# A one-column memset on GpSimd between each two additions of exponentials in a forgetting-attention kernel, their order pinned

## The chip, the cores and the metric

The kernel runs on one core of one Trainium2 chip. The metric is the device time of one execution in microseconds (us); a comparison takes the median of several executions. The engines are named as in the profile: PE is TensorE's matmul, PEld its weight load, DVE is VectorE, ACT is ScalarE, POOL is GpSimd, SP is the engine that issues the DMAs.

## The reference, cut to what matters

One decoder layer: forgetting attention with 16 heads of 64 columns, then a gated feed-forward part, then a norm. The change touches the softmax of the attention alone: for each head and each block of queries, `p = softmax(s)` over the keys, and `o = p @ v`.

```python
s = jnp.einsum('bhqd,bhkd->bhqk', q_blk, k).astype(jnp.float32) * (FOX_HEAD_DIM ** -0.5)
s = s + (c_q[..., :, None] - c_k[..., None, :])
s = jnp.where(pos_k[None, :] <= pos_q[:, None], s, -jnp.inf)
p = jax.nn.softmax(s, axis=-1)
return jnp.einsum('bhqk,bhkd->bhqd', p, v.astype(jnp.float32))
```

Each softmax needs the sum of its exponentials over all keys. That sum is what the changed lines form.

## The kernel before

The 1040 positions (1024 and 16 meta tokens) are worked on in three large stages: the attention (to about 700 us), the first feed-forward product (to about 1260 us), and the second with the final norm. Only the attention is touched.

The attention goes by pairs of heads, p = 0 to 7. A pair has two heads e = 0, 1, and the queries are cut into two blocks of 512 columns, c = 0, 1. Keys stand in tiles of 128 partitions, j = 0 to 8; block c = 0 sees 5 of them, block c = 1 all 9, and a tile on the diagonal is narrower than 512 columns (400, 272, 144, 16).

For one head and block the steps are these. `attn_scores` (L342) multiplies keys and queries on PE into PSUM (S, L356 and L357), copies them with a bias on ACT into a tile sb (L363), masks the diagonal part on POOL (the select, L368), and keeps a running maximum rm of the tiles on DVE (L374, L378, L376). `attn_max` (L381) transposes rm on PE (pm, L387), reduces it on DVE (mc, L389) and spreads it again on PE (pb, L392). `attn_exp` (L395) subtracts the maximum on DVE (L398) and takes the exponential on ACT (L399), in place. `attn_out` (L401) multiplies the exponentials by the values on PE (O, L410), and adds the tiles of a head up on POOL:

```python
for i, (j, s, n, sj) in enumerate(tiles[1:]):
    src = total[e] if i else first
    nc.gpsimd.tensor_tensor(total[e][:n, s:], src[:n, s:], sj, ALU.add)
```

These are the additions (L422): 4 of them for each head with c = 0 and 8 with c = 1, so 24 in a pair of heads and 192 in all. Their results, the tiles t (`total`), go to `attn_sum` (L425), which sums them over partitions on PE (Z, L431); `combine_unit` (L465) divides by that sum and multiplies by the gate.

Beside this, PE runs the projections of the next pair (pj, L189 to L195). Their weights come in 512-column pieces (wraw); ACT rounds a piece to its high part wh (L96) and DVE forms the rest, wl = wraw - wh (L98), which PE waits for. In the last pairs the output projection (`oproj`, L477) takes that place: DVE forms the low parts of the weights (wol, L497) and of the attention's output (ob, L490), and PE multiplies them into acca (L504 to L506).

Nothing in the code fixes the order of instructions as a whole: the strings `first`, `steady`, `before` and `final` (L574 to L577) say in which order the steps are recorded, and a scheduler then places every instruction on its engine by its own estimate of when it can start. Each engine works its instructions off in the order so placed. Two means in the code bind the scheduler: `tc.keep_in_program_order` pins an instruction's place relative to others that are pinned, and `tc.issue_after` makes the instructions recorded in its block stand behind a given one on its engine.

Of the kernel before, what the change touches and what calls it, by code (L numbers as in the profile page):

```python
# [8 lines left out]
F32 = mybir.dt.float32  # L9
F32R = mybir.dt.float32r  # L10
AF = mybir.ActivationFunctionType
ALU = mybir.AluOpType
AX = mybir.AxisListType

P = 128
# [20 lines left out]
def fox_block(ctx, tc, hT, hN, wqkvg, w0f, w0g, wo, w1, w2, g_attn, g_ffn, g_fin, g_q, g_k, b_f, out):  # L36
    nc = tc.nc
    PS = bass.MemoryType.PSUM

    cpool = ctx.enter_context(tc.tile_pool(name="cpool", bufs=1))  # L40
# [2 lines left out]
    nc.scalar.preload_act_table_set(ACT_SET)  # L43
    ident = cpool.tile([P, P], F32, tag="ident", name="ident")
    make_identity(nc, ident)
    epsb = cpool.tile([P, 1], F32, tag="epsb", name="epsb")
    nc.gpsimd.memset(epsb, EPS)

# [31 lines left out]
    def bank(tag, name):  # L80
        return ps.tile([P, 512], F32, tag=tag, name=name, bufs=BANKS[tag])
# [29 lines left out]
    def t512(tag, name, dt=F32):  # L111
        return ap_.tile([P, 512], dt, tag=tag, name=name, bufs=BUFS[tag])
# [15 lines left out]
    for k in range(NK):  # L128
# [8 lines left out]
        g = gA[:, k : k + 1]  # L137
# [263 lines left out]
    def attn_out(p, c):  # L401

        st = state[p]
        po = bank("O", f"O{p}_{c}")
        nt = len(st[0, c][0])
        for i in range(nt):
            for e in range(2):
                j, s, n, sj = st[e, c][0][i]
                r = slice(64 * e, 64 * e + 64)
                nc.tensor.matmul(po[r, s:], lhsT=st["V"][:n, j, r], rhs=sj, start=(i == 0), stop=(i == nt - 1))  # L410
        o_t = t512("cmb", f"o{p}_{c}")
        nc.scalar.copy(o_t, po)

        total = st["t", c] = [t512("cmb", f"t{p}_{c}_{e}") for e in range(2)]
        for e in range(2):
            tiles = st[e, c][0]
            first, s1 = tiles[0][3], tiles[1][1]
            if s1 > 0:
                nc.gpsimd.tensor_copy(total[e][:, :s1], first[:, :s1])
            for i, (j, s, n, sj) in enumerate(tiles[1:]):  # L420
                src = total[e] if i else first
                nc.gpsimd.tensor_tensor(total[e][:n, s:], src[:n, s:], sj, ALU.add)  # L422
        st["o", c] = o_t

    def attn_sum(p, c):  # L425
# [153 lines left out]
    for p in range(-1, NK):  # L579
        for op, *a in (first if p < 0 else steady if p + 2 < NK else before if p + 1 < NK else final).split():  # L580
# [6 lines left out]
            elif op == "P":  # L587
                proj_unit(p + 1, *a)
            elif op == "M":
                attn_max(p, *a)  # L590
            elif op == "Z":
                if p >= a[0]:
                    attn_sum(p - a[0], a[1])
            elif op == "N":
                norm_unit(p + 1, *a)
            elif op == "T":
                stack_unit(p + 1, *a)
            elif op == "F":
                forget_unit()
            elif op == "G":  # L600
                gate_unit(p + 1 - int(p + 1 == NK))
            elif op == "W":
                if p + 2 < NK:
                    st_w[p + 2] = stage_w(p + 2)
            elif op == "O":
                attn_out(p, *a)
            elif op == "L":
                combine_load(p, *a)
            elif op == "C":
                if p >= a[0]:  # L610
                    combine_unit(p - a[0], a[1])
            elif op == "A":
                for _ in range(a[1]):
                    next(og[a[0]])
# [487 lines left out]
```

## Time and profile before

| | us |
|---|---|
| runs, lowest / median / highest of 3 | 1440.89 / 1458.1 / 1458.68 |
| the profiled execution | 1449.52 |
| its span, first to last instruction | 1447.9 |
| POOL busy in the span | 448.4 (31%) |
| DVE busy in the span | 1041.0 (72%) |

The profiled execution is one run of its own: 1.6 us of its time lie around the span, and it stands 8.6 us under the median of the three timed runs and 8.6 us over their lowest. The profile tells for each engine when an instruction began and how long it took, and for an idle engine which instruction's end it was waiting for. An instruction that has begun and is held up by something inside the chip shows as a longer duration, not as idle time.

### The profile page before, as it was taken

The numbers are of one execution on the slowest core, as the hardware profiler recorded it, in microseconds if no ns is written. First come the engines' busy times: TensorE is split into PE (matmuls) and PEld (weight loads), VectorE is DVE, ScalarE is ACT, GpSimd is POOL, SyncE is SP. The second block draws the span as 40 slices with busy tenths as digits, with TensorE's granted clock in tenths as the row PEclk, the third lists the DMA queues.
The fourth block names the chain that finished last, engine by engine and source line by source line (L and its number), as shares of the span: only waits on it lengthen the run. The fifth ranks groups of instructions, "written<-read, shape, count | busy, mean of one in ns | idle before, by whom it ended". The sixth has DMA issues, their size and how long they took to land.

```text
span 1447.9 us, 20369 instructions
## 1 busy us (share of the span) xinstructions
PE 1381.0 (95%) x6699; PEld 1115.0 (77%) x6699; DVE 1041.0 (72%) x1819; ACT 679.2 (47%) x1444; POOL 448.4 (31%) x532
## 2 busy tenths in 40 slices
PE   7999999999999999979798999999999999999996
PEld 7887887878787878757576888888888888876874
DVE  7656666777767777677969677666666765798796
ACT  6455555556555565546545233232233323434535
POOL 4021515252432416152404020111111111596182
PEclk9999999999999999999999999999999999999998
DMA  6343425160706142364643232223333228653344
GB/s 200 107 101 92 126 56 154 40 178 19 198 19 176 42 137 74 86 203 143 227 166 124 75 136 88 106 92 109 109 110 109 95 73 301 223 167 100 90 146 146
DMA packets 103196, 178.85 MB, mean 124 GB/s; under 512 B 16553, under 2 KB 25778, under 8 KB 103090
## 3 DMA queue, kind: packets, MB, share of 16 engines
q1 hardware_dynamic: 103090, 177.55, 38.6%
q8 instruction: 53, 0.87, 0.2%
q14 instruction: 53, 0.43, 0.1%
HBM read 109.46 MB, written 38.54 MB: 102 GB/s over the span
## 4 chain that ended last, share of the span: by engine, by line
PE 72%; DVE 13%; DMA 7%; issue 4%; ACT 2%; SPq 1%; POOL 0%; DVEq 0%; ACTq 0%; POOLq 0%
PE f L726 10%; PE f L728 10%; PE f L727 10%; PE pj L193 5%; PE pj L194 5%; PE pj L195 5%; DMA wraw<-wqkvg 5%; PE O L410 3%; PE y L922 2%; PE y L923 2%; PE y L921 2%; PE S L356 2%; PE S L357 2%; PE pg L445 1%; PE pg L446 1%
## 5 line engine op out<-in xcount | busy, mean ns | idle before, releaser
L193 PE MATMUL pj<-wh,xhb 128*128 128x384 f32 (+1 forms) x512 | 176.2, 346 | 7.2 <-ACT xhb L139 5.9
L368 POOL TENSOR_SCALAR_AFFINE_SELECT sb<-sb 128x128 f32<-128x128 f32 (+2 forms) x160 | 58.5, 368 | 390.7 <-ACT sb L363 383.1
L194 PE MATMUL pj<-wl,xhb 128*128 128x384 f32 (+1 forms) x512 | 175.7, 343 | 0.0
L195 PE MATMUL pj<-wh,xlb 128*128 128x384 f32 (+1 forms) x512 | 172.5, 341 | 0.0
L363 ACT ACTIVATE sb<-S,nb 128x512 f32<-128x512 f32 (+4 forms) x224 | 117.0, 538 | 51.9 <-PE S L357 45.9
L422 POOL TENSOR_TENSOR t<-t,sb 128x512 f32<-128x512 f32 (+4 forms) x160 | 136.9, 877 | 0.0
L805 POOL TENSOR_TENSOR gs<-u,u 128x512 f32<-128x512 f32 x11 | 14.1, 1286 | 382.3 <-DVE u L792 382.3
L398 DVE TENSOR_TENSOR sb<-sb,pb 128x512 f32<-128x512 f32 (+4 forms) x224 | 95.7, 497 | 26.6 <-PE pb L392 26.5
L399 ACT ACTIVATE sb<-sb 128x512 f32<-128x512 f32 (+4 forms) x224 | 94.1, 478 | 40.7 <-DVE sb L398 40.6
L193 PEld LDWEIGHTS pj<-wh,xhb 128*128 128x128 f32 x512 | 97.5, 191 | 11.4 <-ACT xhb L139 6.4
L378 DVE TENSOR_TENSOR rm<-rm,sb 128x512 f32<-128x512 f32 (+4 forms) x160 | 87.0, 544 | 20.4 <-ACT sb L363 8.6
L194 PEld LDWEIGHTS pj<-wl,xhb 128*128 128x128 f32 x512 | 97.7, 191 | 4.2 <-issue 2.4
L195 PEld LDWEIGHTS pj<-wh,xlb 128*128 128x128 f32 x512 | 97.1, 190 | 1.5
L410 PE MATMUL O<-sb,V 128*64 128x512 f32 (+4 forms) x448 | 91.9, 463 | 0.0
L356 PE MATMUL S<-Q,K 128*128 128x512 f32 (+4 forms) x224 | 76.2, 344 | 0.7 <-ACT sb L363 0.6
L357 PE MATMUL S<-Q,K 128*128 128x512 f32 (+4 forms) x224 | 71.3, 323 | 0.0
L98 DVE TENSOR_TENSOR wl<-wraw,wh 128x512 fp32r<-128x512 f32 x56 | 48.9, 884 | 30.7 <-ACT wh L96 30.3
L96 ACT CAST wh<-wraw 128x512 fp32r<-128x512 f32 (+1 forms) x64 | 38.5, 607 | 62.7 <-DMA wraw<-wqkvg 32.0
L410 PEld LDWEIGHTS O<-sb,V 128*64 128x64 f32 (+1 forms) x448 | 33.9, 135 | 34.5 <-issue 20.7
L772 DVE TENSOR_TENSOR u<-f,x 128x512 f32<-128x512 f32 x19 | 13.1, 692 | 64.6 <-PE f L728 64.6
L356 PEld LDWEIGHTS S<-Q,K 128*128 128x128 f32 (+1 forms) x224 | 39.5, 176 | 20.7 <-issue 6.5
L374 DVE TENSOR_TENSOR rm<-sb,sb 128x400 f32<-128x400 f32 (+1 forms) x32 | 36.8, 1150 | 24.4 <-ACT sb L363 21.3
(1374 smaller groups left out, 3928.1 us busy)
## 6 DMA issues: line engine op xcount, KB each, us to landing
Q<-tq SPq DMA_DIRECT2D x128, 128.0 KB, 2.3
wraw<-wqkvg SPq DMA_DIRECT2D x56, 256.0 KB, 4.7
av<-w SPq DMA_DIRECT2D x22, 512.0 KB, 3.2
gs<-qs SPq DMA_DIRECT2D x44, 256.0 KB, 2.6
ga<-qa SPq DMA_DIRECT2D x33, 256.0 KB, 3.3
K<-tk SPq DMA_DIRECT2D x64, 128.0 KB, 2.8
wor<-wo SPq DMA_DIRECT2D x32, 256.0 KB, 3.1
a11r<-w SPq DMA_DIRECT2D x22, 256.0 KB, 3.0
```

The lines of the kernel that those rows point to most:

```text
L193: nc.tensor.matmul(o, lhsT=xh[k][:, sl], rhs=wh, start=(k == 0), stop=False)
L194: nc.tensor.matmul(o, lhsT=xh[k][:, sl], rhs=wl, start=False, stop=False)
L195: last_mm[0] = nc.tensor.matmul(o, lhsT=xl[k][:, sl], rhs=wh, start=False, stop=(k == NK - 1))
L356: nc.tensor.matmul(psx[:n, s0:], lhsT=kk[:, j * P : j * P + n], rhs=q[:, 0, s0:], start=True, stop=False)
L357: nc.tensor.matmul(psx[:n, s0:], lhsT=kk[:, j * P : j * P + n], rhs=q[:, 1, s0:], start=False, stop=True)
L363: nc.scalar.activation(sj, psx[:n, s:], AF.Identity, bias=nbias[c][:n, j, head : head + 1], scale=1.0)
L398: nc.vector.tensor_tensor(sj, sj, mx[:n, s:], ALU.subtract)
L410: nc.tensor.matmul(po[r, s:], lhsT=st["V"][:n, j, r], rhs=sj, start=(i == 0), stop=(i == nt - 1))
L422: nc.gpsimd.tensor_tensor(total[e][:n, s:], src[:n, s:], sj, ALU.add)
L726: nc.tensor.matmul(pp, lhsT=s[0][:, ks], rhs=bh, start=(k == 0), stop=False)
L727: nc.tensor.matmul(pp, lhsT=s[0][:, ks], rhs=bl, start=False, stop=False)
L728: nc.tensor.matmul(pp, lhsT=s[1][:, ks], rhs=bh, start=False, stop=(k == 3))
```

## The change

Before each of the 192 additions a memset of one column (128 partitions, one float32 each) is issued on POOL, into a tile `gap` that nothing reads. The memsets are pinned in program order among themselves, and each addition is bound to stand behind its memset.

```diff
+    gap = cpool.tile([P, 1], F32, tag="gap", name="gap")
...
             for i, (j, s, n, sj) in enumerate(tiles[1:]):
                 src = total[e] if i else first
-                nc.gpsimd.tensor_tensor(total[e][:n, s:], src[:n, s:], sj, ALU.add)
+
+                g = tc.keep_in_program_order(nc.gpsimd.memset(gap, 0.0))
+                with tc.issue_after(g.ins):
+                    nc.gpsimd.tensor_tensor(total[e][:n, s:], src[:n, s:], sj, ALU.add)
```

Lines behind the first new one move down by one, lines behind the additions by four: the addition is L426 in the changed kernel, the select L369, wl L98 becomes L99, wol L497 becomes L501, ob L490 becomes L494, rm L374 becomes L375.

The first place is POOL, at the additions of block c = 1 of the first pair of heads. A name t_1_0 is the total of block 1 and head 0, t_1_1 that of head 1; the sb tiles are the exponentials (second input) or, in a select, scores of a later block. In square brackets stand the semaphores that an instruction waits for; Pool_49 is POOL's own. Before:

```order
L422 TENSOR_TENSOR t_1_0_1684<-sb_1_0_1093,sb_1_1_1098 128x512
L422 TENSOR_TENSOR t_1_1_1685<-sb_1_0_1302,sb_1_1_1307 128x512 [waits PE_49]
L422 TENSOR_TENSOR t_1_0_1684<-t_1_0_1684,sb_1_2_1103 128x512 [waits Pool_49]
L368 AFFINE_SELECT sb_0_0_1563<-sb_0_0_1563 128x112 [waits Activation_49]
L422 TENSOR_TENSOR t_1_1_1685<-t_1_1_1685,sb_1_2_1312 128x512 [waits Pool_49]
L368 AFFINE_SELECT sb_0_0_1815<-sb_0_0_1815 128x112 [waits Activation_49]
L422 TENSOR_TENSOR t_1_0_1684<-t_1_0_1684,sb_1_3_1108 128x512 [waits Pool_49]
L422 TENSOR_TENSOR t_1_1_1685<-t_1_1_1685,sb_1_3_1317 128x512 [waits Pool_49]
```

The same place in the changed kernel:

```order
L424 MEMSET gap 128x1
L426 TENSOR_TENSOR t_1_0_1693<-sb_1_0_1094,sb_1_1_1099 128x512
L424 MEMSET gap 128x1 [waits Pool_49]
L426 TENSOR_TENSOR t_1_0_1693<-t_1_0_1693,sb_1_2_1104 128x512 [waits Pool_49]
L424 MEMSET gap 128x1 [waits Pool_49]
L369 AFFINE_SELECT sb_0_0_1572<-sb_0_0_1572 128x112 [waits PE_49,Activation_49]
L426 TENSOR_TENSOR t_1_0_1693<-t_1_0_1693,sb_1_3_1109 128x512 [waits Pool_49]
L424 MEMSET gap 128x1 [waits Pool_49]
L369 AFFINE_SELECT sb_0_0_1840<-sb_0_0_1840 128x112 [waits Activation_49]
L426 TENSOR_TENSOR t_1_0_1693<-t_1_0_1693,sb_1_4_1114 128x512 [waits Pool_49]
```

Before, the two heads' totals alternate, so that an addition waits for the one before the last. Now all eight additions of head 0 come first and then all eight of head 1, and each reads what the addition just in front of it (but for the memset) has written.

The second place is PE, where the sums over partitions of block c = 1 of the second pair of heads stand (Z_1, L431 before and L435 now). Before:

```order
L357 MATMUL S_1_1_2955<-Q_0_1_2702,K_0_2411 128x512
L431 MATMUL Z_1_2853<-t_1_0_2614,one 64x512
L194 MATMUL pj_4_3018<-wl_5_2665,xhb 128x384
L431 MATMUL Z_1_2853<-t_1_1_2615,one 64x512
L356 MATMUL S_1_2_2960<-Q_0_1_2702,K_0_2411 128x512
```

Now, in two pieces with 29 rows between them:

```order
L358 MATMUL S_1_3_3014<-Q_0_1_2751,K_0_2444 128x512
L435 MATMUL Z_1_2902<-t_1_0_2647,one 64x512
L411 MATMUL O_0_3152<-sb_0_0_2526,V_1887 64x512
```

```order
L358 MATMUL S_1_5_3027<-Q_0_1_2751,K_0_2444 128x400
L435 MATMUL Z_1_2902<-t_1_1_2648,one 64x512
L194 MATMUL pj_4_3067<-wh_0_2683,xhb 128x384
```

The sum of head 0 stands 32 rows earlier on PE than before (row 1099 against 1131), that of head 1 four rows earlier (1129 against 1133).

The third place is DVE, near the end of the attention, where the fourth piece of the output projection's weights (wol_0_3) is split. Before:

```order
L490 TENSOR_TENSOR ob_7389<-ogr_3_7559,ob_7389 128x512
L374 TENSOR_TENSOR rm_0_7139<-sb_0_0_7143,sb_0_1_7151 128x400
L378 TENSOR_TENSOR rm_0_7139<-rm_0_7139,sb_0_2_7159 128x272
L497 TENSOR_TENSOR wol_0_3_7566<-wor_0_3_7563,woh_0_3_7565 128x512
L378 TENSOR_TENSOR rm_0_7139<-rm_0_7139,sb_0_3_7167 128x144
```

Now:

```order
L494 TENSOR_TENSOR ob_7558<-ogr_3_7728,ob_7558 128x512
L501 TENSOR_TENSOR wol_0_3_7735<-wor_0_3_7732,woh_0_3_7734 128x512
L375 TENSOR_TENSOR rm_0_7292<-sb_0_0_7296,sb_0_1_7304 128x400
L379 TENSOR_TENSOR rm_0_7292<-rm_0_7292,sb_0_2_7312 128x272
L377 COPY rm_0_7292<-sb_0_0_7296 128x112
```

The split of wol_0_3 stood behind the first two steps of a running maximum and stands in front of them now.

## Rows read from the trace of the kernel before

**Rows 1.** The page, busy time: us, share of the span, instructions.

```profile
PE 1381.0 (95%) x6699; PEld 1115.0 (77%) x6699; DVE 1041.0 (72%) x1819; ACT 679.2 (47%) x1444; POOL 448.4 (31%) x532
```

**Rows 2.** Stretches: length, busy PE, PEld, DVE, ACT, POOL, granted clock, DMA share, GB/s.

```profile
311.00:388.00 77.00, 74.56 (x419) 60.83 (x418) 56.28 (x116) 45.60 (x105) 26.97 (x48) 1.00 0.38 101
625.00:700.00 75.00, 62.69 (x268) 44.54 (x267) 60.06 (x94) 39.19 (x81) 24.42 (x40) 0.93 0.48 161
```

**Rows 3.** Who PE waited for: us in total, times, longest us.

```profile
PE acca L505 <- DVE wol L497: 7.3, 2, 6.8
PE pm L387 <- DVE rm L376: 5.7, 5, 2.0
PE pj L190 <- DVE wl L98: 5.0, 2, 2.6
```

**Rows 4.** Timeline, 620 to 637 us: start us, us, engine, line, idle time before.

```profile
621.00 3.98 DVE L497 TENSOR_TENSOR wol<-wor,woh 128x512 fp32r<-128x512 f32 x1 [0.42 <-ACT woh L496]
...
624.32 0.79 POOL L368 TENSOR_SCALAR_AFFINE_SELECT sb<-sb 128x112 f32<-128x112 f32 x1
...
625.56 1.36 DVE L490 TENSOR_TENSOR ob<-ogr,ob 128x512 fp32r<-128x512 f32 x1
626.33 0.72 POOL L368 TENSOR_SCALAR_AFFINE_SELECT sb<-sb 128x112 f32<-128x112 f32 x1
626.85 8.27 DVE L374 TENSOR_TENSOR rm<-sb,sb 128x400 f32<-128x400 f32 x1
627.03 7.65 POOL L422 TENSOR_TENSOR t<-t,sb 128x512 f32<-128x512 f32 x7
628.61 0.86 PE L504 MATMUL acca<-woh,ob 128*128 128x512 f32 x3
635.22 0.44 DVE L378 TENSOR_TENSOR rm<-rm,sb 128x272 f32<-128x272 f32 x1
635.58 0.69 DVE L497 TENSOR_TENSOR wol<-wor,woh 128x512 fp32r<-128x512 f32 x1
...
636.32 0.80 PE L505 MATMUL acca<-wol,ob 128*128 128x512 f32 x1 [6.85 <-DVE wol L497]
```

**Rows 5.** Running maximum's first step, all of the kernel: duration ns min/median/max.

```profile
L374 DVE TENSOR_TENSOR rm<-sb,sb x32: 555/743/8270, 82.6 to 680.2; 128x400 f32<-128x400 f32 x16, 128x512 f32<-128x512 f32 x16
```

**Rows 6.** Stretch behind that wait, columns as in rows 2.

```profile
634.60:641.40 6.80, 5.08 (x16) 3.86 (x17) 4.22 (x11) 2.43 (x5) 1.39 (x3) 0.50 0.54 189
```

**Rows 7.** Timeline, a projection's weights at 309 and at 468 us.

```profile
309.61 1.88 DVE L374 TENSOR_TENSOR rm<-sb,sb 128x400 f32<-128x400 f32 x1
...
311.41 3.22 DVE L98 TENSOR_TENSOR wl<-wraw,wh 128x512 fp32r<-128x512 f32 x1
311.60 2.48 POOL L422 TENSOR_TENSOR t<-t,sb 128x512 f32<-128x512 f32 x2
...
314.69 0.39 PE L190 MATMUL pj<-wl,xtail 128*128 128x256 f32 x1 [2.44 <-DVE wl L98]
...
468.54 3.23 DVE L98 TENSOR_TENSOR wl<-wraw,wh 128x512 fp32r<-128x512 f32 x1
...
471.82 0.39 PE L190 MATMUL pj<-wl,xtail 128*128 128x256 f32 x1 [2.55 <-DVE wl L98]
```

**Rows 8.** POOL, a memset of one column, and a chain of dependent operations.

```profile
L47 POOL MEMSET epsb<- 128x1 f32 x1 | 0.1, 99 | 0.0
...
982.52 1.29 POOL L805 TENSOR_TENSOR gs<-u,u 128x512 f32<-128x512 f32 x1 [33.70 <-DVE u L792]
983.89 1.29 POOL L807 TENSOR_TENSOR u<-x,u 128x512 f32<-128x512 f32 x1
```

**Rows 9.** Timeline, a pair's last addition and its sums, and an addition held up.

```profile
231.27 1.73 POOL L422 TENSOR_TENSOR t<-t,sb 128x512 f32<-128x512 f32 x1
...
324.40 0.21 POOL L422 TENSOR_TENSOR t<-t,sb 16x16 f32<-16x16 f32 x1
...
328.13 1.08 PE L431 MATMUL Z<-t,one 128*64 128x512 f32 x4
```

## The prediction, made before the changed kernel ran

> **What bounds the kernel now.** I read the busy times first, then the stretches, then who PE waited for, and last the timeline around the longest of those waits. PE is busy 95% of the span and POOL, which the change loads, 31% [rows 1]. In a pair of heads in the steady part (311 to 388 us) PE works 74.6 of 77 us while POOL works 27.0 [rows 2]: PE sets the time there, and POOL could take on much before it did. Only the last stretch of the attention, 625 to 700 us, is different: PE works 62.7 of 75 us, and its granted clock falls to 0.93 on average [rows 2]. So the change can gain only where PE stands idle because of POOL's additions, and lose only where PE begins to wait for them.
>
> The list of waits names three that matter: PE waited 7.3 us for wol, 6.8 of it at once; 5.0 us for wl, in two waits; 5.7 us for rm, in five [rows 3]. All three producers are DVE operations with both inputs in SBUF. The timeline shows why the first was late. At 626.85 DVE began a first step of a running maximum that takes 0.56 us at its fastest and 0.74 in the median [rows 5], and it took 8.27 us. Over the same time POOL ran seven additions without a pause, 627.03 to 634.68 [rows 4]. When they ended, DVE ended, at 635.12. The split of wol_0_3 stood two rows behind it on DVE, ended at 636.27, and PE, out of other work since 629.47, went on at 636.32 [rows 4]. PE's wait is put down to that split alone.
>
> So an addition on POOL holds up a DVE operation that reads two tiles from SBUF, and a run of additions can hold it up for the whole run. The same happened three additions deep at 621.00 (3.98 us, let in when the select at 624.32 came) [rows 4], and two deep at 311.41 and 468.54 (3.22 and 3.23 us, where 0.69 is the unhindered split of wol in rows 4, of the same shape); PE stood 2.44 and 2.55 us for those two [rows 7]. Where only one addition stood in the way, the delay was one addition: the maximum at 309.61 took 1.88 us [rows 7].
>
> [...]
>
> **The change part by part.** *POOL's own time.* 192 memsets come in. One of one column shows 0.10 us [rows 8], so 19 us at most. The additions also become dependent ones: before, the two heads' totals alternated; now each addition waits for the one in front of it. The price of that shows in the feed-forward part, where L807 overwrites a tile that L805 reads and so waits for it: from the start of the one to that of the other it is 983.89 - 982.52 = 1.37 us [rows 8], against 2.48 / 2 = 1.24 for the two at 311.60 [rows 7], so 0.13 us. The pause between the two is 983.89 - 983.81 = 0.08 us, and a memset that waits only for the memset before it can run in it. I take 0.13 us an addition; the bounds are 0 and 0.23 (0.13 + 0.10). That is 24 x 0.13 = 3.1 us of POOL in a pair, 25 us in all, at most 44. POOL has 50 us idle in a pair [rows 2], so it costs nothing by itself; it costs where something waits for a pair's last addition, which is the third rival.
>
> *The long hold-up at 627 us.* The pause behind every addition, with or without the memset in it, is what DVE lacked. Besides, the split of wol_0_3 now stands in front of the running maximum on DVE. If DVE is let in after one addition at most, the split, which DVE could begin at 626.92, ends by 626.92 + 1.28 + 0.69 = 628.9, before PE runs out of work at 629.47. The idle 6.85 us goes whole. Next in line on DVE is the maximum itself, at most 1.9 us, which nothing on PE waits for as soon. Value: 6.8 us, with 0 as the other end if DVE is not let in.
>
> *The clock behind it.* [...] Value: 2.5 us, from 0 to 3.4 (half the stretch).
>
> *The two splits of wl.* With one addition in the way each would take 0.69 + 1.28 = 1.97 us, not 3.22: 1.25 us saved twice, 2.5 us; the bounds are 0 and the whole idle time, 5.0.
>
> *The waits for rm.* They are waits for single additions for the most part, which a memset does not shorten. Value 0, from a gain of 5.7 (all of them) to a loss of the same size, since a lengthened run of additions can also meet more of DVE's operations.
>
> *The order elsewhere.* The scheduler has placed most of the attention anew. PE has the same instructions; PE's busy time does not move, only its idle time, of which there are 2.4 us in that pair [rows 2]. I take 0.
>
> Sum: 6.8 + 2.5 + 2.5 = 11.8 us off the profiled execution's 1449.5 us gives 1438 us. That execution is 8.6 us under the median of the three timed runs, and 8.6 over the lowest. As the hold-ups depend on which of two engines comes first, I read the runs' spread as hold-ups that are longer in some executions, and the lowest, 1440.9, as one with little of them. So 1438 is forecast for the median too: 1.4% under 1458.1.
>
> **The rivals.** *DVE is held as before.* If DVE is let in only by an operation that pauses POOL for longer (a select, a wait for ACT), the memset and the wait of 0.08 us change nothing. For it: each of the holds at 621.00, 311.41 and 468.54 ended at a select or where POOL waited for one. Against it: the additions were then back to back with no pause at all, as 7.65 us for seven shows. The time would be 1449.5 to 1458, the kernel of before; I put it at 1452, the new place of wol_0_3 having some worth still.
>
> *More is gained.* If DVE also gets in earlier for rm, up to 5.7 us of those waits and 2.5 more of wl go: 1438 - 8 = 1430. For it: the selects stand earlier among the additions now, so rm's inputs are masked sooner. Against it: one addition must still be waited for.
>
> *PE waits for the sums.* Slower than before. The sums of a pair begin 328.13 - 324.61 = 3.5 us after the last addition [rows 9], and the second now stands four rows earlier on PE, some 0.8 us at the 0.2 us of a row. So 2.7 us are left, and 16 dependent additions take 2.1 of them at my price, 3.7 at the upper one. Each time DVE gets in, the next addition is held: 1.73 against 1.28 us [rows 9], 0.45. If that happens for half the additions, it is 3.6 us more. Then PE waits 3.7 + 3.6 - 2.7 = 4.6 us in each of the seven pairs that are followed by another, 32 us, less the 11.8 gained: 1470 us. It decides from a growth of 2.7 us in a run of sixteen additions. Against it: DVE's operations do not become more, and those of before held POOL up as well (231.27); the sum of head 0 has its half of the additions done far earlier.
>
> **How the numbers follow.** 1438 as summed: 0.55. Held as before, 1452: 0.18. More gained, 1430: 0.14. PE waits for the sums, 1470: 0.13. The likeliest's own range is 1432 to 1447. The range for 8 in 10 runs from 1427, under the case with more gained, to 1460, over the case of no effect; most of the slow case is left out. A measurement of this kernel can tell about 2% from no change: faster means under 1428.9, slower over 1487.3. Half of the case with more gained and a trifle of the main case lie below: 0.08. A quarter of the slow case lies above: 0.03. Within 2%: 0.89.
>
> **What would show it.** Right: no DVE operation over about 2.2 us in the attention; no wait of PE for wol near 630 us and no clock of 0.50 behind it; the list of PE's waits without 7.3 us for wol and with about half the 5.0 for wl; 192 memsets on POOL with the step from one wide addition to the next near 1.37 us. Wrong: a DVE operation as long as several additions (held as before), or PE waiting for POOL in front of the sums of L435 (the slow case), or new idle time of PE of more than 10 us at another line, by the new order alone.

## The result, and the profile after

The changed kernel ran in 1461.9 us (median of 17 runs, 1460.06 to 1467.1), the kernel before on the same chip in 1450.96 (17 runs, 1437.11 to 1460.64). The ratio is 1.0082, with a 95% interval of 1.0062 to 1.0101: slower by 0.8%, where 1.4% faster was forecast and 1460 was the upper end of the range. The profiled execution took 1461.3 us, its span is 1459.6: 11.7 us more than that of before.

The lines of after stand one further on than those of before up to the additions (now L426, the memset L424), and four further on behind them. First the busy times on the page of after, which answer to [rows 1]:

```profile
PE 1398.8 (96%) x6699; PEld 1118.5 (77%) x6699; DVE 1042.4 (71%) x1819; ACT 674.2 (46%) x1444; POOL 461.8 (32%) x724
```

PE has the same 6699 instructions and is busy 17.8 us longer; its idle time in the span falls by 6.1 us, and the two make the 11.7. The loss is in PE's busy time. The stretches, columns as in [rows 2]:

```profile
311.00:388.00 77.00, 76.75 (x413) 60.79 (x415) 55.60 (x114) 43.11 (x101) 28.93 (x68) 1.00 0.36 95
625.00:700.00 75.00, 67.27 (x300) 47.88 (x296) 57.30 (x86) 40.99 (x85) 41.42 (x82) 0.95 0.57 176
```

In the steady pair PE was idle 2.44 us before and is idle 0.25 us now, and does six instructions fewer in the same 77 us (419 and 413). The list of who PE waited for begins, below one wait for ACT, with these:

```profile
PE pm L388 <- DVE rm L379: 5.6, 9, 0.9
PE accb L508 <- DVE h L514: 4.2, 1, 4.2
```

The 7.3 us for wol and the 5.0 for wl of [rows 3] are gone from it. The tiles' durations (ns, min/median/max) say the same: nothing in the attention is held for a run of additions any more, where [rows 5] had 8270. The longest DVE operation between 80 and 720 us takes 2.18 us.

```profile
L375 DVE TENSOR_TENSOR rm<-sb,sb x32: 559/672/1253, 80.1 to 679.4; 128x400 f32<-128x400 f32 x16, 128x512 f32<-128x512 f32 x16
...
L501 DVE TENSOR_TENSOR wol<-wor,woh x32: 672/684/1778, 618.4 to 754.2; 128x512 fp32r<-128x512 f32 x32
...
L99 DVE TENSOR_TENSOR wl<-wraw,wh x56: 672/692/1757, 47.4 to 553.4; 128x512 fp32r<-128x512 f32 x56
```

The timeline of POOL and DVE shows how DVE gets in:

```profile
236.23 1.26 POOL L426 TENSOR_TENSOR t<-t,sb 128x512 f32<-128x512 f32 x1
236.25 2.38 DVE L379 TENSOR_TENSOR rm<-rm,sb 128x144 f32<-128x144 f32 x2
...
237.44 0.10 POOL L424 MEMSET gap<- 128x1 f32 x1
237.57 1.03 POOL L426 TENSOR_TENSOR t<-t,sb 128x400 f32<-128x400 f32 x1
```

The addition ends at 237.49, the next starts at 237.57, and in that pause of 0.08 us the held DVE operation is let in (the first of its two ends at 237.66). So the hold-ups went as forecast. What came instead is in the Z matmuls. In the kernel before, the four instructions of the Z at 328.13 took 1.08 us [rows 9]; 6 of its 16 Z are of this kind, and 3 of 16 in after. The PE timeline of after has the same Z two and two, 7.6 us apart, and each two take as long as the four did:

```profile
326.50 1.04 PE L435 MATMUL Z<-t,one 128*64 128x512 f32 x2 [0.25 <-DVE sb L399]
...
334.11 1.07 PE L435 MATMUL Z<-t,one 128*64 128x512 f32 x2
```

A Z matmul is 128*64 in its row, half of the 128*128 of pj, and so is an O matmul; in the code head 0 of each writes rows 0 to 63 of the result and head 1 rows 64 to 127. Where the two heads' Z stand side by side, both run in the time of one: four instructions in 1.08 us, against 1.04 and 1.07 for the two of one head. Matmuls that run beside each other need not be of one kind; in the kernel before, an O and a Z start within 0.01 us of each other:

```profile
359.56 0.64 PE L410 MATMUL O<-sb,V 128*64 128x512 f32 x1
359.57 0.64 PE L431 MATMUL Z<-t,one 128*64 128x512 f32 x1
```

Going through all 512 instructions of O and Z by their starts, I count those that have no other of them starting within 0.03 us: 214 before, 252 after (of Z 26 and 50). The count gives a narrow O the weight of a full Z, so the time is the better measure: O and Z together, each moment counted once, fill 110.8 us of PE before and 122.8 after. The pinned order caused that: before, the additions of the two heads alternated and both totals were ready together; now head 0's total is ready eight additions before head 1's, and the scheduler placed its Z as soon as that.

The other part is the clock. After has seven stretches at half clock (granted 0.50) between 80 and 810 us, 30.7 us in all; before had four, 17.1 us. Two new ones lie where before had none. Ahead of the first, PE waited three times within 4 us, each time for one more step of the running maximum, as DVE is now let in behind an addition but then meets the next one (from 154.09 three of these steps take 2.84 us on DVE, with additions from 154.33 to 155.79 and from 155.87 to 156.90 on POOL):

```profile
154.26 0.33 PE L388 MATMUL pm<-ident,rm 128*128 128x128 f32 x1 [0.90 <-DVE rm L377]
...
156.01 0.33 PE L388 MATMUL pm<-ident,rm 128*128 128x128 f32 x1 [0.79 <-DVE rm L379]
...
156.98 0.33 PE L388 MATMUL pm<-ident,rm 128*128 128x128 f32 x1 [0.47 <-DVE rm L379]
```

and the stretch itself, columns as in [rows 2]:

```profile
157.20:160.60 3.40, 3.40 (x13) 3.40 (x13) 1.99 (x3) 2.19 (x5) 3.40 (x9) 0.51 0.27 104
```

An account of the span can be made of three terms: PE's busy time less half of what lay at half clock (its work at full clock, by estimate: in the stretch at 157.2 matmuls pj of 128x384 start 0.32 us apart, and behind it 0.17), that half, and PE's idle time, which is the span less its busy time. Before: 1371.9 + 9.1 + 66.9. After: 1383.8 + 15.0 + 60.8. So +11.9 of work, +5.9 by the clock and -6.1 idle make the 11.7 us. O and Z alone fill 12.0 us more, 0.6 of it by the clock.

### The profile page after: what moved, and what is told of

It is laid out like the page before. It is cut to its first block, busy times and chain, and to the rows that moved or that the text cites. A ratio compares the mean times of both kernels' runs of the same rounds, so it can differ in the third digit from the quotient of the medians.

```text
span 1459.6 us, 20564 instructions
## 1 busy us (share of the span) xinstructions
PE 1398.8 (96%) x6699; PEld 1118.5 (77%) x6699; DVE 1042.4 (71%) x1819; ACT 674.2 (46%) x1444; POOL 461.8 (32%) x724
## 4 chain that ended last, share of the span: by engine, by line
PE 70%; DVE 13%; DMA 6%; issue 5%; ACT 3%; SPq 2%; POOL 0%; DVEq 0%; POOLq 0%; ACTq 0%
PE f L732 10%; PE f L731 10%; PE f L730 10%; PE pj L194 5%; PE pj L195 5%; PE pj L196 5%; PE O L411 4%; DMA wraw<-wqkvg 2%; PE y L926 2%; PE y L927 2%; PE y L925 2%; PE S L357 2%; PE Z L435 2%; PE S L358 2%; DVE rm L379 1%
## 5 line engine op out<-in xcount | busy, mean ns | idle before, releaser
L369 POOL TENSOR_SCALAR_AFFINE_SELECT sb<-sb 128x128 f32<-128x128 f32 (+2 forms) x160 | 55.8, 356 | 358.1 <-ACT sb L364 350.4
L426 POOL TENSOR_TENSOR t<-t,sb 128x512 f32<-128x512 f32 (+4 forms) x160 | 144.7, 905 | 4.4
L379 DVE TENSOR_TENSOR rm<-rm,sb 128x512 f32<-128x512 f32 (+4 forms) x160 | 111.7, 698 | 38.5 <-POOL sb L369 16.1
L411 PE MATMUL O<-sb,V 128*64 128x512 f32 (+4 forms) x448 | 93.7, 466 | 0.5 <-ACT sb L400 0.5
L99 DVE TENSOR_TENSOR wl<-wraw,wh 128x512 fp32r<-128x512 f32 x56 | 40.9, 736 | 26.2 <-ACT wh L97 25.8
L210 ACT ACTIVATE sq<-pj 128x256 f32<-128x256 f32 x64 | 24.5, 383 | 54.3 <-PE pj L196 43.8
```

What stands on the lines that cost most here:

```text
L379: nc.vector.tensor_tensor(rm[:n, s:], rm[:n, s:], sj, ALU.max)
```

## The experiments

Theory: (1) the order head by head tears pairs of half-width matmuls on PE; (2) DVE is let in where POOL pauses, which an addition does that waits for the one in front, and not because of a memset. The first holds in the main; of the second, the runs bear out only that a pause is enough. Rivals: the memsets' own time, a lengthened run of additions, or the memset as what lets DVE in. Medians; the ratio is against the kernel before on the same chip, whose medians were 1455.0 (E1 to E5), 1455.4 (E6 to E8) and 1453.8 us (E9 to E11). "Held" is the longest DVE operation from 80 to 720 us, "alone" the count of 512 from above, and the last three are the terms of the account. Terms and holds are those of the one profiled execution, which can lie off the median: E8's was the fastest of its twelve (1457.8 us) and E7's the slowest (1457.7).

| kernel | additions | us | ratio, interval | held | alone | work + clock + idle |
|---|---|---|---|---|---|---|
| before | alternating | 1451 to 1455 | 1 | 8.27 | 214 | 1371.9 + 9.1 + 66.9 |
| after | by head, memset | 1461.9 | 1.0082, 1.0062 to 1.0101 | 2.18 | 252 | 1383.8 + 15.0 + 60.8 |
| E2 | by head, no memset | 1472.4 | 1.0124, 1.0085 to 1.0163 | 3.20 | 208 | 1378.9 + 19.2 + 73.8 |
| E4 | as after, Z bound together | 1453.7 | 0.9999, 0.9975 to 1.0023 | 1.88 | 170 | 1380.1 + 8.2 + 63.2 |
| E8 | as E2, Z bound together | 1462.8 | 1.0034, 1.0012 to 1.0055 | 3.27 | 184 | 1372.1 + 13.6 + 70.4 |
| E1 | alternating, memset | 1448.8 | 0.9953, 0.9924 to 0.9982 | 8.53 | 200 | 1367.3 + 12.2 + 63.3 |
| E7 | as E1, wait for the memset | 1453.9 | 1.0000, 0.9974 to 1.0027 | 1.77 | 192 | 1374.7 + 15.6 + 65.7 |
| E5 | alternating, pinned, no memset | 1472.8 | 1.0131, 1.0081 to 1.0181 | 12.64 | 214 | 1371.3 + 19.0 + 82.1 |
| E6 | as E5, wait for the addition in front | 1452.2 | 0.9977, 0.9949 to 1.0005 | 2.51 | 192 | 1370.0 + 16.5 + 66.3 |
| E9 | before, all O and Z bound in pairs | 1451.6 | 0.9988, 0.9954 to 1.0023 | 9.60 | 42 | 1358.2 + 21.1 + 72.6 |
| E10 | E1, all O and Z bound in pairs | 1448.1 | 0.9971, 0.9941 to 1.0000 | 2.53 | 6 | 1354.9 + 21.4 + 69.4 |
| E11 | before, Z bound together | 1487.2 | 1.0232, 1.0178 to 1.0287 | 11.37 | 202 | 1362.9 + 29.7 + 88.3 |

**The order and the memset by themselves: E2, E4, E8.** E2 takes the memset out of the changed kernel and keeps the order.

```diff
-                g = tc.keep_in_program_order(nc.gpsimd.memset(gap, 0.0))
-                with tc.issue_after(g.ins):
-                    nc.gpsimd.tensor_tensor(total[e][:n, s:], src[:n, s:], sj, ALU.add)
+                tc.keep_in_program_order(nc.gpsimd.tensor_tensor(total[e][:n, s:], src[:n, s:], sj, ALU.add))
```

> The order head by head stays pinned, but the memsets are left out: each addition waits for the one in front of it and nothing stands between. 8 of the 16 pairs of Z matmuls stand apart on PE, against 13 in the changed kernel and 3 by two rows before. Theory that the torn Z pairs cost the time: PE time of Z about 23 to 26 us, time about 1452 to 1460 us. If the pause behind a dependent addition is what lets DVE in, no DVE operation is held for two or more additions and the spread is as narrow as in the changed kernel; if the memset is needed for that, DVE operations of 3 us and more come back and the runs spread over 10 us and more. Rival (the memsets cost the time): 1440 to 1448 us.

E4 leaves the changed kernel as it is and binds head 0's Z behind head 1's; E8 does so in E2.

```diff
-            for e in range(2):
-                nc.tensor.matmul(pz[64 * e : 64 * e + 64], ..., rhs=total[e], start=True, stop=True)
+            z1 = nc.tensor.matmul(pz[64:128], ..., rhs=total[1], start=True, stop=True)
+        with tc.issue_after(z1.ins):
+            nc.tensor.matmul(pz[0:64], ..., rhs=total[0], start=True, stop=True)
```

> The changed kernel with one thing altered: the Z matmul of head 0 is bound to stand behind that of head 1 on PE, so that all 16 pairs stand side by side; POOL's order and its memsets stay. Theory of the torn Z pairs: PE time of Z 17 to 18.5 us, about 10 us less than in the changed kernel, and a time of 1448 to 1454 us. Rival (POOL's longer runs or the memsets): Z now waits for the later total, PE idles in front of it, and the time stays at 1459 to 1468 us.

> The order of the changed kernel and the Z matmuls of the two heads bound together, as in E4, without the memsets: it gives the memset's own worth against E4 (1453.7 us), and the tearing's against E2 (1472.4 us, same additions, Z pairs torn). If torn Z pairs cost about 10 to 12 us, this kernel comes to 1460 to 1463 us, with Z at 16 us of PE instead of 25.6. If the memset closes what is left (holds over 3 additions where a select stands between two dependent ones, 14 us in E2, none in E4), E4 stays 5 to 9 us ahead of it. The rival, that E2's time came from its holds and not from the torn pairs: 1470 us or more, with Z pairs together all the same.

In E4's PE timeline the two heads' Z, now two lines, start together:

```profile
330.27 0.64 PE L434 MATMUL Z<-t,one 128*64 128x512 f32 x1
330.27 0.64 PE L436 MATMUL Z<-t,one 128*64 128x512 f32 x1
```

The four kernels make a square. Binding the Z takes 8.2 us off with the memset (1461.9 to 1453.7) and 9.6 without it (1472.4 to 1462.8); by the ratios 12 and 13. In E4 O and Z fill 114.1 us of PE, 8.7 less than in after; in E8 110.6, 10.7 less than in E2. So theory 1 holds for the time of O and Z, and the kernel gains each time. But the gain does not come by that time alone: from after to E4 the work as a whole falls by only 3.7 us, as other matmuls take longer (O by itself fills 97.2 us against 93.7), while the clock gives 6.8 back and the idle time grows by 2.4. Why the clock fell less often in E4 is not shown. E2 was expected at 1452 to 1460 us and came 12 us above that. The memset takes 10.5 us off where the Z are torn and 9.1 where they stand together; by the ratios 6 and 5. So the memset is worth something in this order. What is missing without it is seen in E2, where a select stands between two additions, and the second then starts without a pause:

```profile
321.45 4.68 DVE L379 TENSOR_TENSOR rm<-rm,sb 128x272 f32<-128x272 f32 x2 [0.19 <-POOL sb L369]
321.57 1.29 POOL L424 TENSOR_TENSOR t<-sb,sb 128x512 f32<-128x512 f32 x1
322.82 0.28 POOL L369 TENSOR_SCALAR_AFFINE_SELECT sb<-sb 128x128 f32<-128x128 f32 x1
323.08 1.27 POOL L424 TENSOR_TENSOR t<-t,sb 128x512 f32<-128x512 f32 x1
324.31 0.39 POOL L369 TENSOR_SCALAR_AFFINE_SELECT sb<-sb 16x16 f32<-16x16 f32 x1
324.67 2.64 POOL L424 TENSOR_TENSOR t<-t,sb 128x512 f32<-128x512 f32 x2
```

The first of the two DVE operations took 3.20 us; it got in behind the second addition, at the second select, and not at the first. E2 has five such holds and E8 six, where the longest in after is 2.18 us and in E4 1.88.

**What lets DVE in: E1 against E7, E5 against E6.** E1 keeps the memsets and lets the two heads' additions alternate, so that an addition no longer waits for the one just in front. E5 is E1 without the memsets.

```diff
+        heads = [(total[e], st[e, c][0]) for e in range(2)]
...
+        for i in range(1, nt):
+            for t, tiles in heads:
+                j, s, n, sj = tiles[i]
+                src = t if i > 1 else tiles[0][3]
...
                 g = tc.keep_in_program_order(nc.gpsimd.memset(gap, 0.0))
                 with tc.issue_after(g.ins):
-                    nc.gpsimd.tensor_tensor(total[e][:n, s:], src[:n, s:], sj, ALU.add)
+                    nc.gpsimd.tensor_tensor(t[:n, s:], src[:n, s:], sj, ALU.add)
```

> The memsets stay, before each addition, but the two heads' additions alternate again as before the change, so that both totals are ready together and the two heads' sums over partitions (Z) stand side by side on PE in 15 of 16 cases. Theory (PE lost time because the pinned order, head by head, tore the two heads' Z matmuls apart, and a pair that stands together runs at the same time on the two halves of the columns): the PE time of Z falls from 27.9 us to 17 to 18.5 us, no DVE operation of the attention is held for two or more additions, and the time is 1438 to 1446 us against 1451 before, with a spread of a few us. Rival (the memsets themselves, or POOL's longer runs of additions, cost the time): it stays at 1457 to 1465 us.

> The alternating order of E1 pinned, without memsets: POOL's additions stand as before the change. It tells the memset's own worth apart from the pinning. If the memset is what breaks DVE's long waits, this one has DVE operations held for two and more additions again and runs spread over 10 us and more around 1448 to 1455 us, 8 us or so over E1; if the pinning alone had removed them, it equals E1 within 2 us.

In E7 an addition of E1 waits for its memset to be done, in place of only standing behind it; in E6 an addition of E5 waits for the one in front, in place of the pin. The lines are those of E7.

```diff
+WAIT = mybir.DependencyInfo(mybir.DependencyClass.Sync, mybir.DependencyReason.DATA)
...
+                tc.add_manual_dep(a.ins, g.ins.name, WAIT, reason="the memset in front")
```

> As E1 (alternating, a memset in front of each addition), but the addition waits for the completion of its memset. E1 and this kernel have the same work and the same number of memsets; only the wait is new. Theory A (the pause lets VectorE in): E1's hold of 8.5 us over 7 additions with 7 memsets between is gone, the longest hold is under 3 us, Z stays at about 16 us, and the time is 1437 to 1446 us. Theory B (the memset itself lets VectorE in, and E1's long hold had another cause): holds as in E1, about 1449 us. Against the kernel with the wait alone (without memset), it should differ by less than 4 us, if all that the memset adds is GpSimd time that lies beside other work.

> The two heads' additions alternate as in E5, without a memset, but every addition now waits for the completion of the one in front of it, of the other head. Theory A (a pause between two additions on POOL lets a held VectorE operation in; where the additions stream there is none): no hold of a VectorE operation over more than 3 additions, where E5 had two over 11; the holds that are left end where a select stands between two additions. The Z pairs stand together on PE, so Z takes about 16 us of PE as in E1 and PE's busy time is about 1380 us. PE no longer waits 9 us for a weight load. By E1's span less its 7.2 us wait this gives a time of 1437 to 1445 us against about 1455 of the kernel before. Theory B (it is the memset as an instruction of its own that lets VectorE in): the holds are those of E5, over 10 additions, and the time is that of E5, about 1470 us. Theory C (the additions' own pace decides, and waits of 0.07 us on 182 additions make the sums late): PE waits for Z for over 5 us, and the time is 1460 us or more.

E1 came 3 us above the range of its theory, with a hold that the theory had excluded, and E5 18 us above its own. E1's timeline of DVE, POOL and the PE wait shows a memset between each two additions, no pause, and a DVE operation held over seven of them:

```profile
619.66 8.53 DVE L375 TENSOR_TENSOR rm<-sb,sb 128x400 f32<-128x400 f32 x1
619.83 0.09 POOL L425 MEMSET gap<- 128x1 f32 x1
619.89 1.29 POOL L427 TENSOR_TENSOR t<-t,sb 128x512 f32<-128x512 f32 x1
621.12 0.09 POOL L425 MEMSET gap<- 128x1 f32 x1
621.18 1.27 POOL L427 TENSOR_TENSOR t<-t,sb 128x512 f32<-128x512 f32 x1
...
627.01 0.75 POOL L427 TENSOR_TENSOR t<-t,sb 128x272 f32<-128x272 f32 x1
...
629.40 0.79 PE L510 MATMUL acca<-wol,ob 128*128 128x512 f32 x1 [7.17 <-DVE wol L502]
```

The addition of 619.89 ends at 621.18, where the next starts. Elsewhere in E1 a DVE operation does get in at such a place, with a memset and no pause:

```profile
306.95 3.61 DVE L99 TENSOR_TENSOR wl<-wraw,wh 128x512 fp32r<-128x512 f32 x2 [1.21 <-ACT wh L97]
307.01 1.28 POOL L427 TENSOR_TENSOR t<-sb,sb 128x512 f32<-128x512 f32 x1
308.25 0.09 POOL L425 MEMSET gap<- 128x1 f32 x1
308.30 1.70 POOL L427 TENSOR_TENSOR t<-t,sb 128x512 f32<-128x512 f32 x1
```

The first of these two took 1.90 us and ended at 308.85, 0.55 us behind the end of the addition. In E7, with the wait, the last part of the attention reads:

```profile
626.98 0.10 POOL L426 MEMSET gap<- 128x1 f32 x1
627.15 1.56 POOL L427 TENSOR_TENSOR t<-sb,sb 128x512 f32<-128x512 f32 x1
627.51 1.76 DVE L503 TENSOR_TENSOR wol<-wor,woh 128x512 fp32r<-128x512 f32 x1
628.66 0.09 POOL L426 MEMSET gap<- 128x1 f32 x1
```

One addition, then DVE is in: 1.77 us is the longest in E7. The other pair has its long holds only without the wait. E5 in the steady part, where the first of the two DVE operations took 12.64 us, and below it the sum of such waits of PE:

```profile
310.22 13.24 DVE L99 TENSOR_TENSOR wl<-wraw,wh 128x512 fp32r<-128x512 f32 x2 [0.90 <-ACT wh L97]
...
314.72 7.59 POOL L425 TENSOR_TENSOR t<-t,sb 128x512 f32<-128x512 f32 x7
...
322.92 0.58 PE L191 MATMUL pj<-wl,xtail 128*128 128x256 f32 x1 [9.30 <-DVE wl L99]
```

```profile
PE pj L191 <- DVE wl L99: 21.2, 5, 9.4
```

and the same two views of E6:

```profile
309.10 2.51 DVE L376 TENSOR_TENSOR rm<-sb,sb 128x400 f32<-128x400 f32 x1
...
309.88 2.86 POOL L427 TENSOR_TENSOR t<-t,sb 128x512 f32<-128x512 f32 x2
```

```profile
PE pj L192 <- DVE wl L100: 2.6, 3, 1.2
```

So the holds are shorter with the wait both times: 12.64 against 2.51 us and 8.53 against 1.77. The wait is not the only difference, since it takes the place of the pin in E6 and of the order behind the memset in E7, and the scheduler places the rest anew. A count over all twelve traces says more. I take each held DVE operation (rm, wl, wol and ob with two inputs, 80 to 720 us) at each end of an addition that another addition follows. Where that next one starts 0.08 to 0.12 us later, DVE got in 175 times of 175. Where it starts at once, DVE got in 88 times of 186 without a memset between, and 54 times of 65 with one. So a pause was enough every time, but it is not the only way in; what decides where there is no pause is not shown. The memset without a pause is not without worth either: E1 and E5 differ by it, and E1 is 24 us faster (by the ratios 26), with 18.8 us less idle time. Whether the memset does that itself or through the order that comes with it, no run separates.

In time the wait gains only from E5 to E6, by 20.6 us. E6 and E7 came 7 to 8 us above the upper end of what was expected. E7 lost E1's hold and its wait of 7.17 us, and PE's idle time is 2.4 us more all the same: the many short waits for rm grew from 6.1 us in seven to 10.7 in sixteen. The work of PE stands 7.4 us higher, in an execution that was the slowest of E7's twelve against a fast one of E1 (1444.9). The price of what a finer interleaving brings had been left out.

**The pairs by themselves: E9, E10, E11.** Here the additions are those of the kernel before (E9, E11) or of E1 (E10). In E9 and E10 each O matmul of head 0 is bound behind that of head 1, as well as Z; E11 has the Z edit of E4 alone.

```diff
+            held = ExitStack()
+            for e in (1, 0):
...
+                with held:
+                    m = nc.tensor.matmul(
+                        po[r, s:], lhsT=st["V"][:n, j, r], rhs=sj, start=(i == 0), stop=(i == nt - 1)
+                    )
+                held = tc.issue_after(m.ins)
```

> The kernel before, its additions untouched; only the order on PE is bound: each O matmul of head 0 comes right behind that of head 1, and so do the two Z matmuls. In the profile of the kernel before 214 of the 512 instructions of O and Z run without one of the other head beside them, and these take 52.6 us of PE; in the changed kernel it is 252 and 70.9 us. Theory (two matmuls of 64 columns, one of each head, run at the same time when they stand side by side, and what the change lost is such pairs): nearly all pairs run together, half of the 52.6 us goes, PE's busy time falls from 1381 to some 1355 us, and the time by 15 to 25 us, to 1430 to 1440 us, if PE does not wait more for the exponentials of head 1. Rival (Z and O pairs are not what PE's busy time rose by, and the 12 us between the changed kernel and E4 came from elsewhere): PE busy at 1381 us as before, the time within 5 us of the kernel before.

> E1 (memsets kept, the two heads' additions alternating) with the same binding of all O and Z pairs on PE. In E1 200 instructions of O and Z run alone, for 48.3 us: by the theory 24 us of PE's busy time go (1379 to about 1355 us), and the time comes to 1425 to 1435 us. As a version for use it should beat the kernel before and the changed one. Rival: no change in PE's busy time, 1449 us.

> The kernel before with the two Z matmuls of a pair bound together and nothing else. Of its Z matmuls 26 of 64 instructions run alone. If pairs on PE are worth what rows show (0.5 us for an instruction that finds its partner), some 12 to 24 instructions find one and PE's busy time falls by 3 to 6 us; the holds of VectorE stay as they are, so the time falls by no more than that, 1449 to 1455 us. Rival (binding the sums does harm by making the first wait): slower than the kernel before.

The first half of the theory holds. O and Z together fall from 110.8 to 96.5 us in E9, and the work at full clock by 13.7; in E10 by 12.4 against E1. The time does not follow, and comes out where the rivals of E9 and E10 had put it: idle and clock take it back (E10: +6.1 idle and +9.2 by the clock against E1), with waits of PE for the exponentials in E10, and for a DVE operation behind a hold of 9.60 us in E9. E11 came out on its rival's side, but not by the rival's reason: no wait for the sums stands in its list. Its work is 9.0 us less than in the kernel before, and it is 2.3% slower, by 21.4 us of idle time and 20.6 by the clock, since binding the Z moved the rest of the order so that weights on DVE fall in front of whole runs of additions four times. One of them in the timeline:

```profile
231.74 11.37 DVE L98 TENSOR_TENSOR wl<-wraw,wh 128x512 fp32r<-128x512 f32 x1 [1.32 <-ACT wh L96]
...
234.97 7.58 POOL L422 TENSOR_TENSOR t<-t,sb 128x512 f32<-128x512 f32 x7
...
243.16 0.58 PE L190 MATMUL pj<-wl,xtail 128*128 128x256 f32 x1 [8.85 <-DVE wl L98]
```

the sum of those waits of PE, and the stretch behind this one (columns as in [rows 2]):

```profile
PE pj L190 <- DVE wl L98: 34.0, 5, 9.0
```

```profile
238.60:248.80 10.20, 5.64 (x21) 5.54 (x22) 7.62 (x11) 2.02 (x5) 3.96 (x5) 0.50 0.19 54
```

A hold of 11 us goes with 9 us of idle time, and then with 10.2 us at half clock in which PE worked for 5.6. E9, E10 and E11 thus cut PE's work by 9 to 14 us, each against the kernel that it changes (E10: E1), and gained nothing: less work in pairs is not by itself less time. The version to use is E1: it is the only one whose whole interval lies ahead of the kernel before, by 0.5%; E10's reaches 1.

## Why the prediction was wrong

The step that failed is "The order elsewhere": "PE has the same instructions; PE's busy time does not move, only its idle time ... I take 0." The same instructions took 17.8 us more: 11.9 of work and 5.9 by the clock. The work rose by O and Z matmuls of 64 columns that lost the partner they had run beside: the two together fill 12.0 us more of PE. E4 takes 8.7 of that back by putting the Z side by side again, and with it the kernel is no slower than before (0.9999), in part by the clock. The rows for it were there: four Z instructions in 1.08 us [rows 9], and 128*64 in their shape. The gains that the prediction looked for came in the main, and none of its three signs of being wrong did: no DVE operation as long as several additions, 0.8 us of wait in front of the sums, no new idle time of over 10 us. No sign had been set on PE's busy time.

*The long hold at 627 us* (-6.8): right. Its wait is gone, and no DVE operation is held over a run. Two reasons had been given, the pause and the new place of wol_0_3, and no run separates them there. The pause "with or without the memset in it" was half of the truth: E2 shows that the dependency without the memset leaves holds where a select comes between, and E1 that the memset without a wait leaves a long one.

*The two splits of wl* (-2.5): right in sign, and more than forecast: the whole 5.0 us left the list.

*The clock behind the hold* (-2.5): wrong in sign. No run shows the 2.5 us as a gain; in its place, the stretch from 634.6 to 641.4 [rows 6] went, but one of half its length stands at 641.9, and others came, +5.9 in the account. Those at 157.2, 239.2 and 641.9 us each come behind three short waits for rm.

*The waits for rm* (0): they hang on two lines, a step of the maximum and a copy. The copy, L376 in [rows 3], has one input, not two as the prediction says of all three producers. Before, the second line beside that of [rows 3], and after, likewise beside the one above:

```profile
PE pm L387 <- DVE rm L378: 2.2, 3, 1.0
```

```profile
PE pm L388 <- DVE rm L377: 1.5, 3, 0.9
```

Their sum hardly moved (7.9 to 7.1 us); their number went from eight to twelve, and that was not priced.

*POOL's own time* (0): right that it is hidden. A run of sixteen additions grew from 19.1 to 19.9 us to between 21 and 25, pair by pair by 1.3 to 5.9 us and in two of six by more than the 2.7 us from which "PE waits for the sums" was to decide, and yet PE waited only 0.8 us in front of Z (L435). The last sums began 1.8 to 5.0 us behind the last addition before, and 1.9 to 3.2 after: their place had moved with the runs, where that rival's point was worked out from the old distance.

*The spread*: the runs agree with it in part. Those of the kernel before spread over 23.5 us and E5's over 21.8; after, without holds, over 7.0, and E7 over 6.6. But E1, with a hold of 8.53 us, spreads over only 8.9, so it is not shown that the spread belongs to the holds.

Open is how much of the half-clock time belongs to which wait, why E4's clock term fell, and why E7's work on PE is 7.4 us above E1's; no run separates these.

## What to carry to other kernels

Before costing a new order at nothing on the busiest engine, look for instructions of half its width (128*64 beside 128*128 here): who stands beside them is part of their price (four Z instructions side by side took 1.08 us, two by themselves 1.04), and a dependency that makes one partner ready early tears the pair. To let VectorE in between additions on GpSimd, make each wait for the one in front; where nothing else stands between them, that bounded a hold at about one addition here (1.77 us the longest in E7, an addition there 1.56), but it splits one long stall into many short ones (7.17 us at once in E1, sixteen waits for rm with 10.7 us in E7), so price both. And in a kernel whose order a scheduler places, even binding two instructions can move the rest by more than it gains (E11, +33 us).

## What the runs showed of the hardware that was not expected

A DVE operation with two inputs in SBUF can stand for ten or eleven additions on POOL, 11.37 us in E11 and 12.64 in E5, and the selects of 0.27 us between the first of these did not let it in. A pause of 0.08 to 0.12 us did every time (175 of 175); without one it got in at 142 of 251 ends of additions. Whether a memset by itself holds DVE up, no run here tests: in E1 a memset begins before the addition in front has ended (621.12 against 621.18), and the next addition starts at that end.

The Z matmuls of the two heads, 128*64 each, run in the time of one where they stand side by side (four instructions in 1.08 us, the two of one head in 1.04). An O and a Z run beside each other too; in the kernel before, an O of 0.64 us and a Z of 0.64 us start at 359.56 and 359.57. And of the clock: three short waits, 0.90, 0.79 and 0.47 us, stood ahead of a stretch at 0.51, where the single wait of 2.44 us in [rows 7] was followed by none (granted 1.00 in [rows 2]).
